# The first block of a second feed-forward as one paired product with two sevens, small loads behind a weight product, and five small groups of instructions a step later

## The chip, the cores and the metric

One core of one Trainium2 chip runs the kernel. The metric is the device time of one execution in microseconds (us): the median of repeated runs, 2222.22 us for the kernel before. The engines are written as the profile writes them: PE (matmul), PEld (weight load), DVE (vector), ACT (scalar), POOL (GpSimd) and SP (the queue that issues most DMAs). L345 is line 345 of the kernel before unless the text says otherwise.

## The reference, cut to what matters

A decoder layer on 256 tokens of width 2048 in fp32: a feed-forward (FFN1), a mixer of windowed attention and a recurrent branch, a cross-attention, a second feed-forward (FFN2), a final norm.

```python
def rms_norm(x, g):
    y = x * lax.rsqrt(jnp.mean(x * x, axis=-1, keepdims=True) + NORM_EPS)
    return y * g
def swiglu(h, w_gate, w_up, w_down):      # h 256x2048, gate and up 2048x5632, down 5632x2048
    return (jax.nn.silu(h @ w_gate) * (h @ w_up)) @ w_down
...
x = x + 0.5 * swiglu(rms_norm(x, g_ffn2), w_gate, w_up, w_down)
```

What the change touches most is the first 512 columns of `h @ w_gate` and `h @ w_up` of FFN2.

## The kernel before, in words

**Matmuls.** Every fp32 operand is split in two parts, hi (a cast on ACT, L345) and lo (what the cast left over, a subtraction on DVE, L346). One product of 128 rows takes three matmuls (`times`, L438 to L440): hi with xhi, lo with xhi, hi with xlo. The tokens stand in two halves t = 0, 1.

**Items.** A weight comes in items of 2 x 128 rows and 512 columns (`items`, with k = 2q the first row block). A plain item is 12 matmuls. A paired item carries the same rows of gate and up: 24 matmuls. `load` issues an item's DMA on SP, `divide` splits it, `next_item` loads up to `LOADED` ahead and divides up to `AHEAD` = 2 item costs ahead (a paired item costs two). The tiles hi and lo have 3 buffers each, so a cast waits until the item three tiles back has left PE. A raw tile is narrow (128x2x512, `raw`, 4 buffers) where no large pool is open, or wide (`raw2`, 128x4x512, `RAW` = 3 buffers).

**Sevens.** In some paired items (`SEVEN`) the eight products of the 2x2 block scheme become seven: 21 matmuls instead of 24. For that DVE forms sums of weights (`sums`, L365 to L367: one 128x1024 and two 128x512), ACT and DVE split them (thi L370 and tlo L371, twice each, 128x1024), and DVE and ACT form combinations c of the activations (`combinations`: u L470 and L475 to L480, chi L483, clo L486). After the last seven, DVE adds banks (`end`, L575 to L577), and the last items end with more adds (`finish`).

**Order of the work.** One Python program emits the instructions of all engines. Beside the weight stream run background generators in named groups (`Interleave`): a `tick` after each product advances each group by one step, and `idle(n)` skips n steps. A scheduler then fixes the order in each engine's row; each engine works its row in order. `issue_after(x)` (and `behind_weights`, which uses it) ties an instruction behind another.

**FFN2's opening, before.** Blocks of 512 columns: block 0 is a gate product and then an up product, each of 8 plain items (96 matmuls each), q = 0 to 7. The first four gate items are narrow, since FFN2's pool isn't open when they are loaded. Just ahead of it the cross-attention's output product ends (its matmuls read ochi, oclo), and the norm of its result `x` turns into the operands: `Norm.block` transposes four columns of x on PE (L187), writes xhi on ACT (L689) and xlo on DVE (L690), column by column, and squares x on ACT (`junk`, L698). After the last of four such groups, DVE sums the squares (`ms`, L752, L754) and POOL takes the root (rs, L756). Blocks 1 to 10 are paired with sevens (`gate_up`). Combinations c start when all of x is done.

**The five small groups.** In the attention: the sum of the softmax (`den`), and the point from which the transposed probabilities go on (the idle ahead of `pt`). In the recurrent branch: the decays' sigmoid chain (an idle of 4), the substitution that inverts a triangular matrix (`xt`, `tmp`, L1247 to L1255, on DVE and ACT), and the block inverse after it (n from ACT, L1388, feeds matmuls at L1351).

## Time and profile before

| | |
|---|---|
| three runs, median (lowest to highest) | 2222.22 us (2221.36 to 2223.51) |
| profiled execution | 2222.56 us |
| its span | 2220.8 us (1.76 us lie around it) |
| granted PE clock | 0.999 |
| matmuls recorded on PE | 10774 |
| bytes read from and written to HBM | 419.00 and 12.45 MB |

The span is one execution. In the lines of the timeline the first number is the start in us from the span's start, the second the duration in us, and brackets hold the idle time of that engine ahead of the instruction and what released it. Matmuls overlap: each record is some 0.39 us long, but the next starts 0.23 us later.

### The profile page before, as it was taken

What the parts mean: (1) busy time and instruction counts of PE and PEld (TensorE: products, weight loads), DVE (VectorE), ACT (ScalarE), POOL (GpSimd) and SP (SyncE); (2) the same over time, 40 slices, a digit from 0 to 9 for tenths busy, and PEclk for the clock granted to TensorE, in tenths of its full rate; (3) what the DMA queues carried; (4) which work ended last, traced back from release to release, by engine and by line L of the source; (5) the groups of instructions that cost most, each with busy time, mean ns of one, the idle gap of its engine ahead of it and who ended that gap; (6) DMA issues with size and microseconds to landing.
All of it is one profiled execution on the core that took longest, in us unless ns stands there. A gap on an engine that the chain in (4) does not pass through costs nothing.

```text
span 2220.8 us, 28313 instructions
## 1 busy us (share of the span) xinstructions
PE 2207.0 (99%) x10774; PEld 1817.7 (82%) x10774; DVE 1759.2 (79%) x2047; ACT 1193.8 (54%) x1438; POOL 72.0 (3%) x140
## 2 busy tenths in 40 slices
PE   9999999999999999999999999999999999999998
PEld 7788888888888877888888888888888888888886
DVE  8988988898887477878546576558888988898887
ACT  6555555555555557534434455456555555555554
POOL 1000000000000000010400000000000000000000
PEclk9999999999999999999999999999999999999999
DMA  7565665565556545677714665557565565565564
GB/s 266 200 219 193 204 208 190 190 209 192 206 183 217 169 131 159 210 226 224 203 55 146 229 219 202 187 168 259 199 204 184 200 209 190 189 208 193 205 207 154
DMA packets 220536, 433.31 MB, mean 195 GB/s; under 512 B 13952, under 2 KB 16336, under 8 KB 220400
## 3 DMA queue, kind: packets, MB, share of 16 engines
q1 hardware_dynamic: 213200, 410.70, 55.6%
q0 software_dynamic: 6624, 20.14, 2.9%
q8 instruction: 84, 1.38, 0.2%
q10 hardware_dynamic: 576, 0.66, 0.1%
q14 instruction: 52, 0.43, 0.1%
HBM read 419.00 MB, written 12.45 MB: 194 GB/s over the span
## 4 chain that ended last, share of the span: by engine, by line
PE 96%; DVE 1%; issue 1%; ACT 1%; DMA 0%; POOLq 0%; POOL 0%; SPq 0%; ACTq 0%; DVEq 0%
PE acc L438 21%; PE acc L439 20%; PE acc L440 20%; PE two L438 9%; PE two L439 9%; PE two L440 9%; PE two L187 2%; PE two L179 1%; DVE lo L346 1%; PE two L1351 0%; PE acc L1488 0%; PE acc L1453 0%; PE acc L1470 0%; PE two L1568 0%; PE acc L1351 0%
## 5 line engine op out<-in xcount | busy, mean ns | idle before, releaser
L345 ACT CAST hi<-raw 128x1024 fp32r<-128x1024 f32 (+1 forms) x769 | 764.0, 1003 | 794.3 <-PE two L440 370.6
L346 DVE TENSOR_TENSOR lo<-raw,hi 128x1024 fp32r<-128x1024 f32 (+1 forms) x770 | 884.2, 1158 | 325.0 <-ACT hi L345 323.7
L438 PE MATMUL acc<-hi,xhi 128*128 128x512 f32 (+1 forms) x1224 | 477.9, 391 | 1.1 <-ACT hi L345 0.7
L439 PE MATMUL acc<-lo,xhi 128*128 128x512 f32 (+1 forms) x1224 | 474.9, 388 | 0.9 <-DVE lo L346 0.9
L440 PE MATMUL acc<-hi,xlo 128*128 128x512 f32 (+1 forms) x1224 | 473.8, 387 | 0.0
L438 PEld LDWEIGHTS acc<-hi,xhi 128*128 128x128 f32 x1224 | 229.6, 188 | 53.3 <-issue 3.9
L439 PEld LDWEIGHTS acc<-lo,xhi 128*128 128x128 f32 x1224 | 229.8, 188 | 49.7 <-DVE lo L346 3.7
L440 PEld LDWEIGHTS acc<-hi,xlo 128*128 128x128 f32 x1224 | 229.8, 188 | 46.3 <-DVE xlo L712 0.2
L371 DVE TENSOR_TENSOR tlo<-raw,thi 128x1024 fp32r<-128x1024 f32 x160 | 193.1, 1220 | 0.0
L370 ACT CAST thi<-raw 128x1024 fp32r<-128x1024 f32 x160 | 165.8, 1051 | 33.4 <-DVE raw L365 19.1
L439 PE MATMUL acc<-lo,hhi 128*128 128x512 f32 x424 | 166.4, 392 | 0.0
L440 PE MATMUL acc<-hi,hlo 128*128 128x512 f32 x424 | 165.1, 389 | 0.0
L438 PE MATMUL acc<-hi,hhi 128*128 128x512 f32 x424 | 159.8, 391 | 0.1
L438 PE MATMUL two<-hi,xhi 128*128 128x512 f32 x352 | 138.4, 393 | 0.0
L439 PE MATMUL two<-lo,xhi 128*128 128x512 f32 x352 | 137.1, 390 | 0.0
L440 PE MATMUL two<-hi,xlo 128*128 128x512 f32 x352 | 137.0, 389 | 0.0
L365 DVE TENSOR_TENSOR raw<-raw 128x1024 f32<-128x1024 f32 x80 | 97.6, 1220 | 14.9 <-DMA raw<-in_ffn_w_up_dram 13.1
L439 PEld LDWEIGHTS acc<-lo,hhi 128*128 128x128 f32 x424 | 79.6, 188 | 19.3 <-DVE lo L346 3.1
L438 PEld LDWEIGHTS acc<-hi,hhi 128*128 128x128 f32 x424 | 79.1, 188 | 18.8 <-ACT hi L345 2.6
L440 PEld LDWEIGHTS acc<-hi,hlo 128*128 128x128 f32 x424 | 79.6, 188 | 16.3
L438 PEld LDWEIGHTS two<-hi,xhi 128*128 128x128 f32 x352 | 66.1, 188 | 15.0 <-DVE u L590 0.5
L440 PEld LDWEIGHTS two<-hi,xlo 128*128 128x128 f32 x352 | 66.1, 188 | 13.9
(392 smaller groups left out, 3190.2 us busy)
## 6 DMA issues: line engine op xcount, KB each, us to landing
raw<-in_ffn_w_gate_dram SPq DMA_DIRECT2D x171, 512.0 KB, 3.7
raw<-in_ffn_w_up_dram SPq DMA_DIRECT2D x167, 512.0 KB, 4.6
raw<-in_ffn_w_down_dram SPq DMA_DIRECT2D x152, 512.0 KB, 4.7
raw<-in_w_in_dram SPq DMA_DIRECT2D x136, 512.0 KB, 3.5
raw<-in_w_out_dram SPq DMA_DIRECT2D x32, 512.0 KB, 3.6
raw<-in_ffn_w_down_dram SPq DMA_DIRECT2D x12, 1024.0 KB, 5.1
raw<-in_w_proj_attn_dram SPq DMA_DIRECT2D x16, 512.0 KB, 3.6
raw<-in_w_proj_rwkv_dram SPq DMA_DIRECT2D x16, 512.0 KB, 4.2
```

The source lines that it names most:

```text
L179: prev = pe.matmul(to, lhs, rhs, **how)
L187: prev = pe.transpose(to, src, ident[:])
L345: newest["act"] = act.copy(hi[:, s], raw[:, s])
L346: newest["dve"] = dve.tensor_tensor(lo[:, s], raw[:, s], f32(hi[:, s]), ALU.subtract)
L365: dve.tensor_tensor(ta[:], raw[:, 1:3], raw[:, 0:2], ALU.subtract)
L370: act.copy(hi[:, s], t[:])
L371: dve.tensor_tensor(lo[:, s], t[:], f32(hi[:, s]), ALU.subtract)
L438: pe.matmul(o, xh, hi, start=first, stop=False, **how)
L439: pe.matmul(o, xh, lo, start=False, stop=False, **how)
L440: newest["pe"] = pe.matmul(o, xl, hi, start=False, stop=last, **how)
```

## The change

Six edits:

1. FFN2's block 0 becomes one paired product (`opening`) over gate and up in the order q = 1, 3, 5, 0, 6, 2, 7, 4, with sevens at q = 0 and 2. Its first item is loaded as two narrow tiles, all others as raw2. The combinations for FFN2 start without the six idle steps, in the order 0, 2, 4, 1, 3, with single idle steps.
2. `load` takes wide tiles whenever a pool is open, which also turns eight narrow loads of the mixer's first weight product into four wide ones.
3. `late_vectors` issues its three small DMAs inside `issue_after` of the newest matmul.
4. The attention: `den` a step later in one of its blocks, and another condition for idle 5 or 4 ahead of `pt`.
5. The decays' idle is 3 instead of 4; the copy of `tmp` (96x1024 on ACT) is split in two halves with a step between.
6. A step more after n in the block inverse.

```diff
+OPENING, SEVEN_OPENING = (1, 3, 5, 0, 6, 2, 7, 4), (0, 2)
@@ feed_forward_plan
-            if j == 0 and together:
-                yield (wg, wu), 0, KD, (0, 0), ()
-            elif j == 0:
-                for w in (wg, wu):
-                    yield w, 0, KD, 0, 512
+            if j == 0:
+                yield (wg, wu), 0, KD, (0, 0), () if together else SEVEN_OPENING
@@ late_vectors
+        with tc.issue_after(newest["pe"].ins):
+            pool.dma_start(gains[:], a["g_later"])
...
@@ load
+        if paired(i) and at["pool"] is None:
+            rows = slice(k * P, (k + KU) * P)
+            raws[i] = []
+            for v, c in zip(w, c0):
+                raw = wp.tile([P, KU, 512], F32, tag="raw", name="raw", bufs=4)
+                nc.sync.dma_start(
+                    raw[:], v[rows, c : c + 512].rearrange("(a p) n -> p a n", p=P)
+                )
+                raws[i].append(raw)
+            return
...
-        wide = at["pool"] is not None and (i < ends[0] or i >= ends[1] + LOADED)
+        wide = at["pool"] is not None
@@ combinations
-            for q in sorted(seven + early):
+            for q in seven + early if soon else sorted(seven + early):
...
-                yield from idle(2)
+                yield from idle(1 if soon else 2)
@@ product_pair
-        for q in range(late + 1):
+        for q in order:
@@ opening (new; product_pair calls after, end and finish)
+        def after(b):
+            act.copy(hb[:, 0], b["p1"])
+        def end(b):
+            dve.tensor_tensor(u[:, 0], b["p6"], hb[:, 0], ALU.add)
+            dve.tensor_tensor(u[:, 1], b["p7"], u[:, 0], ALU.add)
+            dve.tensor_tensor(u[:, 0], b["p5"], u[:, 0], ALU.add)
+            dve.tensor_tensor(u4[:], b["p5"], u[:, 1], ALU.add)
+        def finish(to, b):
+            bg.until(lambda: norm.r is not None)
+            t, v = to in ("p4", "p8"), plus[to]
+            if to in ("p2", "p4"):
+                dve.tensor_tensor(hb[:, t], b[to], v, ALU.add)
+                act.activation(hb[:, t], hb[:, t], AF.Silu, scale=norm.r[t])
+            else:
+                dve.tensor_tensor(v, b[to], v, ALU.add)
+                dve.scalar_tensor_tensor(hb[:, t], v, norm.r[t], hb[:, t], ALU.mult, ALU.mult)
+        product_pair(
+            x, c, w, True, SEVEN_OPENING, (), after, end, finish, order=OPENING
+        )
@@ softmax of the attention
-            yield
+            yield from idle(2 if qb and not kvs[0] else 1)
             dve.tensor_reduce(den[:], s3, AX.X, ALU.add)
...
-            yield from idle(5 if nk == 2 and kvs[0] else 4)
+            yield from idle(5 if kvs[0] > 1 else 4)
@@ decays
-                yield from idle(4)
+                yield from idle(3)
@@ after the substitution
-            act.copy(tmp[:96], xt[:96].rearrange("p u t -> p t u"))
+            for t in (slice(0, 16), slice(16, 32)):
+                act.copy(tmp[:96, t], xt[:96, :, t].rearrange("p u t -> p t u"))
+                yield
@@ block inverse
             act.copy(n2_[low].rearrange("p c n t -> p c (n t)"), b[low])
-            yield
+            yield from idle(2)
```

**ACT's row at the opening.** The rows below are ACT's in order. raw without a number is a narrow tile, raw_12262 and its like are wide ones. Before, from the cast of the second gate item (waiting for DMAHW0) to the casts of gate items 4 and 5 (raw_12262):

```order
L345 CAST hi<-raw 128x1024 [waits DMAHW0_49,PE_49]
L689 ACTIVATE xhi<-two,g_later 128x256 [waits DVE_49]
L345 CAST hi<-raw 128x1024 [waits DMAHW1_49,PE_49]
L689 ACTIVATE xhi<-two,g_later 128x256 [waits DVE_49]
L689 ACTIVATE xhi<-two,g_later 128x256 [waits PE_49]
L689 ACTIVATE xhi<-two,g_later 128x256 [waits DVE_49]
L698 ACTIVATE junk,ss<-x_10697 128x512 [waits Activation_49]
L689 ACTIVATE xhi<-two,g_later 128x256 [waits DVE_49]
L698 ACTIVATE junk,ss<-x_10697 128x512 [waits Activation_49]
L345 CAST hi<-raw 128x1024 [waits DMAHW2_49,PE_49]
L689 ACTIVATE xhi<-two,g_later 128x256 [waits DVE_49] x2
L698 ACTIVATE junk,ss<-x_10698 128x512 [waits Activation_49] x2
```

In the changed kernel (L356 is the cast, L734 xhi, L743 the squares), from the cast of the up half of the first item to the two casts of the second (raw_12252):

```order
L356 CAST hi<-raw 128x1024 [waits DMAHW4_49,PE_49]
L734 ACTIVATE xhi<-two,g_later 128x256 [waits DVE_49] x3
L743 ACTIVATE junk,ss<-x_10690 128x512 [waits Activation_49] x2
L734 ACTIVATE xhi<-two,g_later 128x256 [waits PE_49]
L734 ACTIVATE xhi<-two,g_later 128x256 [waits DVE_49] x3
L743 ACTIVATE junk,ss<-x_10691 128x512 [waits Activation_49] x2
L356 CAST hi<-raw_12252 128x1024 [waits DMAHW6_49,DMAHW5_49]
L356 CAST hi<-raw_12252 128x1024 [waits PE_49]
```

Two casts (those of gate items 2 and 3) have left the stretch, and the rest keeps its order: the next cast stands behind the last group's four xhi and two squares in both.

**DVE's row at the same place.** Changed kernel, from the sum of squares on (L797, L799 are ms, L357 lo, L376 to L378 the sums of weights, L382 tlo, L484 to L500 the combinations):

```order
L797 TENSOR_REDUCE ms<-ss 128x2 [waits Activation_49]
L799 TENSOR_SCALAR ms<-ms 128x2 [waits DVE_49]
L357 TENSOR_TENSOR lo<-raw_12252,hi 128x1024 [waits DMAHW6_49,DMAHW5_49,Activation_49]
L357 TENSOR_TENSOR lo<-raw_12252,hi 128x1024 [waits Activation_49]
L484 TENSOR_TENSOR u<-xhi,xlo 128x512
L489 TENSOR_TENSOR u<-u 128x128 [waits DVE_49]
L491 TENSOR_TENSOR u<-u 128x128
L490 TENSOR_TENSOR u<-u 128x128 [waits DVE_49]
L357 TENSOR_TENSOR lo<-raw_12255,hi 128x1024 [waits DMAHW7_49,DMAHW0_49,Activation_49]
L492 TENSOR_TENSOR u<-u 128x128 [waits DVE_49]
L484 TENSOR_TENSOR u<-xhi,xlo 128x512 [waits DVE_49]
L376 TENSOR_TENSOR raw<-raw_12258 128x1024 [waits DMAHW2_49,DMAHW1_49]
```

Before, from the same sum of squares on:

```order
L752 TENSOR_REDUCE ms<-ss 128x2 [waits Activation_49]
L754 TENSOR_SCALAR ms<-ms 128x2 [waits DVE_49]
L346 TENSOR_TENSOR lo<-raw_12262,hi 128x1024 [waits DMAHW3_49,Activation_49]
L346 TENSOR_TENSOR lo<-raw_12262,hi 128x1024 [waits Activation_49]
L470 TENSOR_TENSOR u<-xhi,xlo 128x512
L475 TENSOR_TENSOR u<-u 128x128 [waits DVE_49,Pool_49]
L477 TENSOR_TENSOR u<-u 128x128
L476 TENSOR_TENSOR u<-u 128x128 [waits DVE_49]
L346 TENSOR_TENSOR lo<-raw_12264,hi 128x1024 [waits DMAHW4_49,Activation_49]
L478 TENSOR_TENSOR u<-u 128x128 [waits DVE_49]
```

The two lo behind ms belong to plain items 4 and 5 before, and to the second paired item now; sums of weights, which before came 28 rows behind ms, now come in the tenth row behind it.

**PE's row.** Changed kernel, the end of the opening's first item and the start of its second (L452 to L454 are hi with xhi, lo with xhi, hi with xlo). The matmul that waits for ACT is the 25th of the opening and needs the first cast of raw_12252; the one that waits for DVE needs the first lo of it:

```order
L452 MATMUL acc<-hi,xhi 128x512
L453 MATMUL acc<-lo,xhi 128x512
L454 MATMUL acc<-hi,xlo 128x512
L452 MATMUL acc<-hi,xhi 128x512 [waits Activation_49]
L452 MATMUL acc<-hi,xhi 128x512
L453 MATMUL acc<-lo,xhi 128x512 [waits DVE_49]
L454 MATMUL acc<-hi,xlo 128x512
L453 MATMUL acc<-lo,xhi 128x512
L454 MATMUL acc<-hi,xlo 128x512
```

The eight transposes of the last group of x stand behind nine matmuls of the first item and ahead of 15; before, they stood behind seven matmuls of the gate product, and the matmul that needs the cast of raw_12262 was its 49th.

**Rows that stay.** POOL's three small DMAs of `late_vectors` stand at the same place of POOL's row in both kernels and wait for nothing in either (the named matmul is on another engine). Until the end of FFN1 all rows are the same.

More of the change, by code (lines that the diff above doesn't have):

```diff
@@ L289, in decoder_layer @@
         w, k0, nk, c0, n = entry
-        for q in range(nk // KU):
+        opens = len(ends) > 1 and len(items) == ends[1]
+        for q in OPENING if opens else range(nk // KU):
             items.append((w, k0 + KU * q, c0, n, isinstance(w, tuple) and q in n))
@@ L379, in divide @@
             parts[i] = split_raw(raw, WHOLE)
+        elif isinstance(raw, list):
+            g, u = (split_raw(v, WHOLE) for v in raw)
+            parts[i] = (g[0], u[0]), (g[1], u[1])
         elif items[i][4]:
@@ L399, in next_item @@
             room -= cost(j)
-            if room < 0 or (paired(j) and at["pool"] is None):
+            if room < 0 or (paired(j) and at["pool"] is None and j < ends[0]):
                 break
@@ L448, in multiply, with combinations @@
             )
-    def combinations(sp, x, seven, early, ready, tag, apart):
+    def combinations(sp, x, seven, early, ready, tag, apart, soon=False):
         n = 4 * len(seven) + 2 * len(early)
@@ L494, in combinations, with product_pair @@
         return c
-    def product_pair(x: Act, c, w, four, seven, early, after, end, finish, first=()):
+    def product_pair(x: Act, c, w, four, seven, early, after, end, finish, first=(), order=None):
         pw, _, nk, _, n = plan[at["product"]]
@@ L504, in product_pair @@
         at["product"] += 1
-        b, begun, late = {}, set(), nk // KU - 1
+        b, begun = {}, set()
+        order = order or range(nk // KU)
+        late, ends_seven = order[-1], [q for q in order if q in seven][-1:]
         def bank(to):
@@ L611, in first_block, with opening @@
         product_pair(x, None, w, False, (), (), None, None, finish)
+        return hb
+    def opening(sp, x, c, norm, w):
+        hb, u = (sp.tile([P, 2, 512], F32, tag="hb", name="hb", bufs=2) for _ in range(2))
+        u4 = sp.tile([P, 512], F32, tag="u", name="u", bufs=2)
+        plus = {"p2": hb[:, 0], "p4": u[:, 1], "p3": u[:, 0], "p8": u4[:]}
+        def after(b):
[17 more added lines that the diff above has]
+        )
         return hb
```

30 lines of the change are left out of this document (9 added, 21 removed).

## The prediction

> **What bounds the kernel now.** I read the page's busy times and its chain first, then what PE waits for, then the windows around FFN2's opening, and there the rows of each engine.
>
> ```profile
> PE 2207.0 (99%) x10774; PEld 1817.7 (82%) x10774; DVE 1759.2 (79%) x2047; ACT 1193.8 (54%) x1438; POOL 72.0 (3%) x140
> PE 96%; DVE 1%; issue 1%; ACT 1%; DMA 0%; POOLq 0%; POOL 0%; SPq 0%; ACTq 0%; DVEq 0%
> ```
>
> PE is busy 2207.0 of 2220.8 us, and 96% of the chain is PE. So a matmul less is a gain, and a gap on PE is a loss, one for one. What can be gained from gaps is small:
>
> ```profile
> PE two L187 <- ACT tok L907: 1.0, 2, 0.6
> PE acc L439 <- DVE lo L346: 0.9, 2, 0.6
> PE two L187 <- DVE s L980: 0.6, 1, 0.6
> PE two L1351 <- ACT n L1388: 0.2, 1, 0.2
> ```
>
> These are (total, times, longest) all waits that the five small groups could touch; none lies in FFN2's opening. The opening's own windows (busy times of PE, PEld, DVE, ACT, POOL, then the granted clock):
>
> ```profile
> core 0: us, PE busy (x) PEld busy (x) DVE busy (x) ACT busy (x) POOL busy (x), PEclk, DMA share, GB/s
> 1507.84:1551.40 43.56, 43.56 (x198) 36.16 (x197) 35.23 (x55) 27.53 (x40) 4.31 (x6) 1.00 0.76 270
> 1551.40:1573.20 21.80, 21.80 (x100) 17.64 (x99) 21.12 (x23) 12.56 (x14) 0.00 (x0) 1.00 0.59 200
> ```
>
> PE never stops in either, but DVE has 8.3 us to spare in the opening and 0.7 us in the block behind it, where two sevens lie. The change brings sevens into the opening, so DVE is what I follow.
>
> **Matmuls removed.** The opening falls from 192 to 186 matmuls.
>
> ```profile
> 1507.84 0.39 PE L438 MATMUL acc<-hi,xhi 128*128 128x512 f32 x1
> 1508.52 0.39 PE L438 MATMUL acc<-hi,xhi 128*128 128x512 f32 x1
> 1509.42 1.03 PE L187 MATMUL two<-ident,x 128*128 128x128 f32 x8
> 1510.21 0.48 PE L439 MATMUL acc<-lo,xhi 128*128 128x512 f32 x1
> ```
>
> Three matmuls start 0.68 us apart, 0.227 each: six are -1.36 us. Eight transposes take 0.79 us of PE.
>
> **The first wait it adds.** The opening starts at 1507.84. Before, plain items of 12 matmuls followed, and the cast of item 4 was needed only after 48. Now the first item has 24, and the second item's cast is needed at 1507.84 + 24 x 0.2267 + 0.79 = 1514.07. On ACT that cast still stands behind the last group's four xhi and two squares, and on DVE its lo behind ms:
>
> ```profile
> 1510.50 0.84 ACT L689 ACTIVATE xhi<-two,g_later 128x256 fp32r<-128x256 f32 x2 [1.04 <-PE two L187]
> 1515.55 0.47 ACT L689 ACTIVATE xhi<-two,g_later 128x256 fp32r<-128x256 f32 x1 [1.31 <-DVE xlo L690]
> 1515.92 0.62 ACT L698 ACTIVATE junk<-x 128x512 bf16<-128x512 f32 x1
> 1516.66 0.63 ACT L698 ACTIVATE junk<-x 128x512 bf16<-128x512 f32 x1
> 1517.29 1.98 ACT L345 CAST hi<-raw 128x1024 fp32r<-128x1024 f32 x2
> 1498.08 0.46 ACT L689 ACTIVATE xhi<-two,g_later 128x256 fp32r<-128x256 f32 x1
> 1499.09 0.47 ACT L689 ACTIVATE xhi<-two,g_later 128x256 fp32r<-128x256 f32 x1 [0.55 <-DVE xlo L690]
> ```
>
> ```profile
> 1517.42 0.16 DVE L752 TENSOR_REDUCE ms<-ss 128x2 f32<-128x8 f32 x1 [0.88 <-ACT junk L698]
> 1518.36 2.36 DVE L346 TENSOR_TENSOR lo<-raw,hi 128x1024 fp32r<-128x1024 f32 x2 [0.57 <-ACT hi L345]
> ```
>
> The last transposes now start after nine matmuls, at 1509.88 instead of 1509.42. The first xhi came 1.08 behind them (1510.50), so now 1510.96. Each xhi waits for the xlo ahead of it and starts 1.02 behind the last (1498.08, 1499.09): three steps give 1514.0 for the fourth. From the fourth xhi (1515.55) to the cast (1517.29) it was 1.74: the cast starts at 1515.76 and ends near 1516.8. Its lo began 1.07 behind the cast (1518.36): 1516.83 to 1518.05. That the two casts ahead of it are gone is in this sum. So PE waits 1514.07 to 1516.8, 2.75 us, runs two matmuls, and waits 0.75 more for lo: **3.5 us**. The loads aren't late:
>
> ```profile
> 1491.35 12.72 SPq L334 DMA_DIRECT2D raw<-in_ffn_w_gate_dram  x6
> ```
>
> SP issued six loads (4 MB) from 1491.35 to 1504.1, each as its tile came free. The first four items now (4 MB) wait for the same narrow tiles or for regions that were free before 1504.
>
> **DVE's backlog.** From there DVE has its row to work off. Start to start it takes 1.14 for 1024 columns (1559.61 to 1560.75), 0.60 for 512 (1563.02 to 1563.62):
>
> ```profile
> 1558.28 0.69 DVE L366 TENSOR_TENSOR raw<-raw,raw 128x512 f32<-128x512 f32 x1
> 1559.00 0.69 DVE L367 TENSOR_TENSOR raw<-raw,raw 128x512 f32<-128x512 f32 x1
> 1559.61 1.22 DVE L346 TENSOR_TENSOR lo<-raw,hi 128x1024 fp32r<-128x1024 f32 x1
> 1560.75 2.35 DVE L371 TENSOR_TENSOR tlo<-raw,thi 128x1024 fp32r<-128x1024 f32 x2
> 1563.02 0.68 DVE L346 TENSOR_TENSOR lo<-raw,hi 128x512 fp32r<-128x512 f32 x1
> 1563.62 1.22 DVE L365 TENSOR_TENSOR raw<-raw 128x1024 f32<-128x1024 f32 x1
> ```
>
> I count its row from that first lo (1516.83) to the first tlo of block 1's second seven. 1024 wide: 10 lo of five paired items, 4 each of the opening's two sevens and block 1's first, 2 lo, 3 up to that tlo, 1 hlo, together 28, or 31.9 us. 512 wide: 8 in sums of weights, 3 lo, 8 in combinations, 4 in end, 4 in finish, together 27, or 16.2. Two products with rs at 0.66, twelve subtractions at 0.21 and four operations on 256 columns at 0.34 are 5.2. The sum is 53.3: DVE is there at 1570.1, if it never waits. PE without any wait would need it after 234 matmuls and two sets of transposes: 1507.84 + 53.05 + 1.58 = 1562.5. So PE is held back by at least **7.6 us** there, the 3.5 included. Before, the same tlo ended at 1561.9 and was needed at 1563.8: the margin of 1.9 is what is eaten first. Walking the row item by item, PE stops some ten times for 0.2 to 1.2 us where a lo, a tlo or a bank that the adds of end read comes last, and DVE waits a few tenths for thi; I take **9.0**, with 6.5 and 10.5 as ends (DVE 3% quicker, or PE not making up what it lost between). Behind block 1's second seven DVE, by then freed of combinations and adds, is again ahead of PE, so nothing is given back and nothing more is lost.
>
> **The small groups.** Den a step later shortens the wait for s (0.6) by about 0.3; the idle ahead of pt only moves transposes beside weight matmuls. The waits for lo (0.9) stand ahead of any changed row and stay. The decays' idle moves one block by six matmuls, but the transposes of tok that wait (0.6 of the 1.0) and ACT's sigmoids ahead of them keep their places: 0. The split copy comes one cast earlier, and its first half frees ACT sooner: of the 0.4 left I take 0.3. The step after n: 0.2, and 0.2 for the shorter form switches there. Against it, the substitution's steps on DVE come one lo earlier in a stretch where DVE has nothing to spare:
>
> ```profile
> 985.00:1033.00 48.00, 48.00 (x213) 39.58 (x212) 47.11 (x63) 19.58 (x20) 0.73 (x1) 1.00 0.66 209
> ```
>
> I put 0.2 on that (bounds 0 and 0.9, the room that 47.11 of 48.00 leaves). Sum **-0.8**, bounds -1.8 (all waits listed but the lo) and +0.9. The small loads stand where they stood on POOL and wait for nothing: 0. Four wide loads for eight narrow ones at the mixer: PE waits for no DMA there; 0.
>
> **Sum.** -1.36 + 9.0 - 0.8 = +6.8 us on the profiled 2222.56, which lies 0.34 above the median of the runs shown: 2222.22 + 6.8 = **2229.0 us**.
>
> **Rivals.**
> *The casts keep ahead* (not slower): paired items and sevens run without a gap in block 1 and might here. Place: the 25th and 26th matmul; it needs the first lo of the second item by 1514.5, 3.5 us before the time worked out, and DVE's 53.3 us in 46. For it: block 1's 21.12 of 21.80. Against it: block 1 has no combinations, no opening squares, and starts with its casts done. Price: -1.36 - 0.8, 2220.1; with all the small waits gone 2218.4 or, with what I can't see, below 2217.8. 9%.
> *Only the first wait counts*: while PE stands, DVE catches up, and behind it has margin as before. Price 3.5 - 1.36 - 0.8, 2223.6. Against it: the count of 53.3 starts behind that wait. It holds if DVE's row is 4 us shorter than counted. 14%.
> *The clock falls in the wait*: PE's two waits lie 0.45 us apart, 3.5 us in all. If the granted clock halved for as long, matmuls at 0.45 instead of 0.227 would lose up to 1.75 us more, though DVE's backlog hides some: 2230.8. Against it: the clock is 0.999 over the span; but the longest wait of PE that this trace has is 1.1 us, so it can't exclude it:
>
> ```profile
> PE acc L204 <- POOL ones L199: 1.1, 1, 1.1
> ```
>
> [...] 8%.
>
> **Chances.** My forecast has 69%. The range 2224.8 to 2232.0 leaves out the first rival, most of the second and the tail beyond the clock's. A measurement of this kernel tells about 0.2% (4.4 us) from no change. Slower by more than that, above 2226.7: my forecast, the clock and a little of the second, 79%. Within: 17%. Faster: 4%.
>
> **What would show it.** Right: in the changed trace PE waits some 2.7 us for ACT's hi near 1514 and then 0.7 for DVE's lo; DVE is busy without a gap from 1517 to about 1570 (less what the small groups move the start); more waits for lo and tlo of 0.2 to 1.2 us up to block 1's second seven and none behind it; the clock stays near 1. Wrong: no wait of PE for hi near 1514 (then ACT's chain of xhi is quicker than 1.02 a step); gaps on DVE between 1520 and 1560 (then the count of its row is too long); a wait of SP's loads showing as PE's; waits of the substitution above 1 us around 975 to 1035.

## The result and the profile after

The changed kernel takes 2231.45 us (median of 6, 2228.85 to 2233.13) against 2221.81 us of the kernel before on the same chip (median of 6, 2220.93 to 2223.51): ratio 1.0042, 95% interval 1.0029 to 1.0055, so +9.6 us. The forecast was 2229.0 and its range 2224.8 to 2232.0. Its profiled execution took 2230.7 us, span 2229.0, 8.2 more than the span before.

In what follows "net" is the difference of medians to the kernel before. Line numbers are those of each kernel: in the changed one L356 and L357 are hi and lo, L452 to L454 the three matmuls, L734 and L735 xhi and xlo, L743 junk, L381 and L382 thi and tlo.

The page's busy times and chain, and what PE waits for (total, times, longest), of the changed kernel:

```profile
PE 2209.9 (99%) x10768; PEld 1817.1 (82%) x10768; DVE 1771.4 (79%) x2065; ACT 1198.3 (54%) x1444; POOL 71.3 (3%) x140
PE 93%; DVE 3%; DMA 1%; ACT 1%; issue 1%; SPq 0%; POOLq 0%; POOL 0%; ACTq 0%; DVEq 0%
```

```profile
PE acc L453 <- DVE lo L357: 3.8, 9, 0.8
PE acc L452 <- ACT hi L356: 3.3, 3, 2.5
...
PE two L1386 <- DVE mk L1478: 0.4, 1, 0.4
```

Six matmuls fewer were recorded, and yet PE's busy time rose by 2.9 us: some of its matmuls became slower (records of 0.63 us instead of 0.39 behind the wait for hi below). The waits for lo and hi rose from 1.6 to 7.1 us, and DVE's share of the chain from 1 to 3%. The 1% of DMA in the chain is the kernel's first loads and two single ones at 1650 and 1937, outside the part that the change touches most.

The opening in the timeline, PE first. Its first matmul starts at 1506.37 (1507.84 before). The 24 of the first item end with the row at 1512.52, then PE waits for the second item's hi:

```profile
1506.37 0.39 PE L452 MATMUL acc<-hi,xhi 128*128 128x512 f32 x1
...
1512.52 0.39 PE L454 MATMUL acc<-hi,xlo 128*128 128x512 f32 x1
1515.39 0.99 PE L452 MATMUL acc<-hi,xhi 128*128 128x512 f32 x2 [2.49 <-ACT hi L356]
1516.65 0.80 PE L453 MATMUL acc<-lo,xhi 128*128 128x512 f32 x1 [0.27 <-DVE lo L357]
1517.25 0.63 PE L454 MATMUL acc<-hi,xlo 128*128 128x512 f32 x1
1517.67 0.63 PE L453 MATMUL acc<-lo,xhi 128*128 128x512 f32 x1
```

From 1512.52 to 1515.39 is 2.87, 2.65 more than the usual 0.226; lo costs 0.68 more. Behind that the matmuls start 0.427 apart, at a granted clock of 0.50 (below). ACT and DVE in the same place:

```profile
1512.57 0.47 ACT L734 ACTIVATE xhi<-two,g_later 128x256 fp32r<-128x256 f32 x1 [0.55 <-DVE xlo L735]
1512.94 0.62 ACT L743 ACTIVATE junk<-x 128x512 bf16<-128x512 f32 x1
1513.68 0.63 ACT L743 ACTIVATE junk<-x 128x512 bf16<-128x512 f32 x1
1514.31 2.92 ACT L356 CAST hi<-raw 128x1024 fp32r<-128x1024 f32 x3
```

```profile
1515.37 2.36 DVE L357 TENSOR_TENSOR lo<-raw,hi 128x1024 fp32r<-128x1024 f32 x2 [0.57 <-ACT hi L356]
...
1569.18 2.35 DVE L382 TENSOR_TENSOR tlo<-raw,thi 128x1024 fp32r<-128x1024 f32 x2
```

The fourth xhi and both squares stand ahead of the cast, and DVE's row runs from 1515.37 to the first tlo of block 1's second seven, which starts at 1569.18 and is done at 1570.4. The windows (busy times, then granted clock) show both the wait with its clock and DVE's row:

```profile
1512.70:1515.40 2.70, 0.21 (x2) 0.01 (x1) 0.84 (x4) 2.67 (x7) 0.51 (x1) 1.00 0.41 143
1515.69:1519.11 3.42, 3.15 (x8) 1.97 (x7) 3.38 (x7) 1.55 (x2) 2.05 (x3) 0.50 0.53 159
1519.40:1560.00 40.60, 39.47 (x166) 29.91 (x164) 40.56 (x58) 23.87 (x28) 0.00 (x0) 1.00 0.66 216
```

The granted clock is 0.50 for 3.4 us behind the wait. From 1519.4 to 1560 DVE is busy 40.56 of 40.60 us, and PE, which had no gap there before, loses time in small waits. The last ones of them:

```profile
1557.14 0.50 PE L453 MATMUL acc<-lo,xhi 128*128 128x512 f32 x1 [0.54 <-DVE lo L357]
1560.67 0.50 PE L453 MATMUL acc<-lo,xhi 128*128 128x512 f32 x1 [0.83 <-DVE lo L357]
1562.50 0.33 PE L186 MATMUL two<-ident,hb 128*128 128x128 f32 x1 [0.17 <-DVE hb L652]
```

Behind these no wait belongs to the opening. The matmul that needs the tlo of 1569.18 starts at 1571.51, 1.1 us after that tlo is done, so the lo and the hb above are the last for which DVE held PE back on the opening's account. Summed up over PE's row (each start less the start ahead of it, less the usual distance of that shape, 0.226 for 512 columns), PE loses 4.8 us in the first 20 us of the opening and 5.0 in the next 40; before, 0.1 and 0.5. These two sums are worked out for each kernel below, and together they are called the lost time. A trace shows one execution: without sevens and with the early squares it lies 2.7 us above its kernel's median, with one seven 1.9, in the others at most 1.2 off.

### The profile page after: what moved, and what is told of

Same layout as the page of the kernel before. It is cut to its first block, busy times and chain, and to the rows that moved or that the text cites. A ratio compares the mean times of both kernels' runs of the same rounds, so it can differ in the third digit from the quotient of the medians.

```text
span 2229.0 us, 28322 instructions
## 1 busy us (share of the span) xinstructions
PE 2209.9 (99%) x10768; PEld 1817.1 (82%) x10768; DVE 1771.4 (79%) x2065; ACT 1198.3 (54%) x1444; POOL 71.3 (3%) x140
## 4 chain that ended last, share of the span: by engine, by line
PE 93%; DVE 3%; DMA 1%; ACT 1%; issue 1%; SPq 0%; POOLq 0%; POOL 0%; ACTq 0%; DVEq 0%
PE acc L452 20%; PE acc L453 20%; PE acc L454 20%; PE two L452 9%; PE two L453 9%; PE two L454 9%; PE two L186 2%; DVE lo L357 1%; PE two L178 1%; DMA raw<-in_ffn_w_up_dram 1%; DVE tlo L382 0%; PE two L1386 0%; PE acc L1523 0%; PE acc L1505 0%; PE acc L1488 0%
## 5 line engine op out<-in xcount | busy, mean ns | idle before, releaser
L356 ACT CAST hi<-raw 128x1024 fp32r<-128x1024 f32 (+1 forms) x769 | 762.4, 1001 | 785.8 <-PE acc L454 368.2
L357 DVE TENSOR_TENSOR lo<-raw,hi 128x1024 fp32r<-128x1024 f32 (+1 forms) x770 | 882.4, 1156 | 313.1 <-ACT hi L356 311.8
L452 PE MATMUL acc<-hi,xhi 128*128 128x512 f32 (+1 forms) x1200 | 468.8, 392 | 3.3 <-ACT hi L356 3.3
L453 PE MATMUL acc<-lo,xhi 128*128 128x512 f32 (+1 forms) x1200 | 466.7, 389 | 3.6 <-DVE lo L357 3.4
L454 PE MATMUL acc<-hi,xlo 128*128 128x512 f32 (+1 forms) x1200 | 465.1, 388 | 0.0
L452 PEld LDWEIGHTS acc<-hi,xhi 128*128 128x128 f32 x1200 | 225.2, 188 | 56.1 <-ACT hi L356 5.5
L454 PEld LDWEIGHTS acc<-hi,xlo 128*128 128x128 f32 x1200 | 225.7, 188 | 45.2
L382 DVE TENSOR_TENSOR tlo<-raw,thi 128x1024 fp32r<-128x1024 f32 x164 | 198.0, 1220 | 0.1
L381 ACT CAST thi<-raw 128x1024 fp32r<-128x1024 f32 x164 | 170.0, 1050 | 42.7 <-DVE raw L376 25.6
L454 PE MATMUL acc<-hi,hlo 128*128 128x512 f32 x424 | 165.1, 389 | 0.0
L452 PE MATMUL acc<-hi,hhi 128*128 128x512 f32 x424 | 159.8, 391 | 0.1
L452 PE MATMUL two<-hi,xhi 128*128 128x512 f32 x364 | 143.4, 394 | 0.0
L453 PE MATMUL two<-lo,xhi 128*128 128x512 f32 x364 | 141.9, 390 | 0.0
L454 PE MATMUL two<-hi,xlo 128*128 128x512 f32 x364 | 141.8, 389 | 0.0
L376 DVE TENSOR_TENSOR raw<-raw 128x1024 f32<-128x1024 f32 x82 | 100.1, 1220 | 17.3 <-DMA raw<-in_ffn_w_up_dram 14.9
L452 PEld LDWEIGHTS acc<-hi,hhi 128*128 128x128 f32 x424 | 79.1, 188 | 18.9 <-ACT hi L356 2.6
L454 PEld LDWEIGHTS acc<-hi,hlo 128*128 128x128 f32 x424 | 79.6, 188 | 16.2
L452 PEld LDWEIGHTS two<-hi,xhi 128*128 128x128 f32 x364 | 68.5, 188 | 15.5 <-DVE u L642 0.4
L454 PEld LDWEIGHTS two<-hi,xlo 128*128 128x128 f32 x364 | 68.4, 188 | 14.4
```

The source lines that it names most:

```text
L356: newest["act"] = act.copy(hi[:, s], raw[:, s])
L357: newest["dve"] = dve.tensor_tensor(lo[:, s], raw[:, s], f32(hi[:, s]), ALU.subtract)
L376: dve.tensor_tensor(ta[:], raw[:, 1:3], raw[:, 0:2], ALU.subtract)
L381: act.copy(hi[:, s], t[:])
L382: dve.tensor_tensor(lo[:, s], t[:], f32(hi[:, s]), ALU.subtract)
L452: pe.matmul(o, xh, hi, start=first, stop=False, **how)
```

## The experiments

The theory is the prediction's: **DVE's row** from the second item's lo to block 1's second seven sets the time. The first rival: **the first wait** and, since the trace shows it, **the half clock** behind it, which would cost PE whatever DVE does. The second: the pairing itself costs. For the small groups, the question is whether they give anything.

### The opening without sevens

```diff
-OPENING, SEVEN_OPENING = (1, 3, 5, 0, 6, 2, 7, 4), (0, 2)
+OPENING, SEVEN_OPENING = (1, 3, 5, 0, 6, 2, 7, 4), ()
...
-    def first_block(sp, x, norm, w):
+    def first_block(sp, x, norm, w, order=None):
...
-        product_pair(x, None, w, False, (), (), None, None, finish)
+        product_pair(x, None, w, False, (), (), None, None, finish, order=order)
...
-                hb = opening(sp, norm.x, c, norm, wg) if last else first_block(sp, norm.x, norm, wg)
+                hb = first_block(sp, norm.x, norm, wg, OPENING if last else None)
```

> The changed kernel with the opening paired and in the same order, but with no seven in it: 192 matmuls as before, and DVE without 4 sums of 512, 2 of 1024, 4 tlo and 6 adds of 512 columns, some 13 us. Against the kernel before. Theory (DVE's row sets the loss; without the 13 us it has caught up by 1556, long before 1563, so that only the first wait of 2.7 to 3.2 and its half clock of 0 to 1.5 are left, less 1.5 of the small groups): +1.2 to +3.5 us. Rival one (the pairing, the order or the loads cost, not the sevens): as the changed kernel and six matmuls more, +9.6 + 1.4 = +11.0. Rival two (the first wait is paid again later): near +6. In the trace: the first wait as in the changed kernel, no waits for lo, tlo or banks of over 0.2 between 1520 and 1570, gaps on DVE before 1560.

Measured: 2228.18 us, ratio 1.0029 (1.0018 to 1.0041), net +6.5 (+4.0 to +9.1). The theory's +1.2 to +3.5 is missed. All of PE's waits in the opening and block 1 that its timeline marks:

```profile
1517.03 0.73 PE L452 MATMUL acc<-hi,xhi 128*128 128x512 f32 x2 [2.48 <-ACT hi L356]
1518.28 0.50 PE L453 MATMUL acc<-lo,xhi 128*128 128x512 f32 x1 [0.53 <-DVE lo L357]
1559.58 0.50 PE L452 MATMUL two<-hi,xhi 128*128 128x512 f32 x1 [0.39 <-DVE hb L623]
1561.31 0.50 PE L453 MATMUL acc<-lo,xhi 128*128 128x512 f32 x1 [0.30 <-DVE lo L357]
```

```profile
1519.22:1522.63 3.41, 3.41 (x10) 2.62 (x9) 3.34 (x8) 0.43 (x1) 0.15 (x1) 0.50 0.91 273
1522.40:1540.00 17.60, 17.60 (x79) 14.58 (x78) 14.76 (x26) 9.41 (x12) 0.00 (x0) 0.99 0.79 271
```

As the theory said, DVE has time to spare now (14.76 of 17.60), and PE's small waits of 1520 to 1557 are gone. But the first wait stays. Its half clock lasts 3.4 us, as long as with sevens, but it begins behind the wait for lo and not ahead of it, so none of it is hidden there and it costs 2.0 us instead of 1.5. And two waits near 1560 are left: lost time 5.3 + 1.6, where two sevens lost 4.8 + 5.0. The theory's own terms, the first wait and its half clock, are 5.3 of these 6.9. Of the 3.0 us by which the theory missed its bound, 1.5 are what it credited to the small groups, which alone gave nothing (below); the rest lies in the half clock (2.0 in place of at most 1.5) and in the waits near 1560. Rival two's number, +6, is near, but not its mechanism: only 1.6 us come later. So with DVE ahead PE still loses 6.9 us, and with two sevens 9.8. That would fit two limits side by side, of which the longer counts; the next kernels test it.

### Matmuls in the first wait

Behind the first item's matmuls PE gets 12 more, into a bank that is begun anew later.

```diff
+            if fillers and q == order[0]:
+                bank("p1")
+                xh = x.parts[0][0]
+                for _ in range(fillers):
+                    with tc.issue_after(newest["pe"].ins):
+                        newest["pe"] = pe.matmul(
+                            b["p1"], xh[:, 4, :P], xh[:, 4:6, :].rearrange("p a n -> p (a n)"),
+                            start=True, stop=True,
+                        )
...
-            x, c, w, True, SEVEN_OPENING, (), after, end, finish, order=OPENING
+            x, c, w, True, SEVEN_OPENING, (), after, end, finish, order=OPENING, fillers=12
```

> The changed kernel with 12 matmuls more behind the first item of the opening, into a bank that the later products overwrite from the start, so that PE works on through the first wait and its granted clock has no cause to fall. Nothing is left out. Against the kernel before. Theory (DVE's row sets the time of block 1's second seven, and the 1.5 us that PE loses at half clock lie beside it): as the changed kernel, +9.6, within 0.5. Rival (the half clock adds its time to the end): 1.5 to 1.9 less, +7.7 to +8.1. In the trace: granted clock near 1 from 1512 to 1520 instead of 0.56 to 0.59; by the theory more PE waits for DVE between 1520 and 1570 to make up for it, by the rival the same ones.

Measured: 2231.27 us, ratio 1.0041 (1.0028 to 1.0054), net +9.6, as the changed kernel itself: the theory. The interval (+6.2 to +12.0) holds the rival's +7.7 to +8.1 too, so the trace has to tell. The windows:

```profile
1516.50:1520.00 3.50, 2.97 (x14) 2.40 (x14) 3.46 (x7) 1.46 (x3) 1.67 (x3) 1.00 0.64 186
1520.00:1540.00 20.00, 19.43 (x83) 14.87 (x82) 19.96 (x33) 11.61 (x16) 0.00 (x0) 1.00 0.72 233
```

The clock stays at 1.00, and the lost time in the first 20 us falls from 4.8 to 3.7 (1.0 beside the 12 matmuls' 2.7); in the next 40 it rises from 5.0 to 6.1. What the clock gave, a wait for DVE took: with two sevens the half clock lies beside DVE's row.

### One seven instead of two

```diff
-OPENING, SEVEN_OPENING = (1, 3, 5, 0, 6, 2, 7, 4), (0, 2)
+OPENING, SEVEN_OPENING = (1, 3, 5, 0, 6, 2, 7, 4), (2,)
```

> The changed kernel with one seven in the opening (q = 2) in place of two: three matmuls more (+0.68 us), and DVE without a sum of 1024, two of 512 and two tlo, some 4.6 us. Against the kernel before. Theory (DVE's row sets the loss, one for one as long as it is behind): 9.6 - 4.6 + 0.7 = +5.7 us, bounds +5.0 and +7.0. Rival (the number of sevens isn't what costs, but the adds at their end or the first wait): +9.6 + 0.7 = +10.3. In the trace: the first tlo of block 1's second seven some 4 to 5 us earlier than in the changed kernel (1569.18).

Measured: 2229.31 us, ratio 1.0032 (1.0020 to 1.0044), net +7.1. That is between the two and just above the theory's bound; the interval (+4.4 to +9.8) holds the theory's +5.7 too. In the profiled execution the first tlo of block 1's second seven starts at 1570.63, 62.4 behind the opening's start (1508.26), against 62.8 in the changed kernel, not 4 to 5 us earlier. DVE, with some 4.6 us less to do (the expectation's count), stands still instead:

```profile
1517.00:1540.00 23.00, 22.18 (x89) 17.92 (x90) 21.01 (x35) 12.38 (x15) 2.64 (x4) 0.93 0.65 213
1540.00:1570.00 30.00, 27.93 (x123) 21.82 (x122) 27.71 (x33) 16.33 (x20) 0.00 (x0) 1.00 0.61 206
```

DVE has 4.3 us free in 53, and PE still waits for a lo three times (lost time 5.3 + 3.4, where two sevens lost 4.8 + 5.0). One of DVE's waits is for a load:

```profile
1523.81 1.22 DVE L357 TENSOR_TENSOR lo<-raw,hi 128x1024 fp32r<-128x1024 f32 x1 [0.79 <-ACT hi L356]
1531.86 1.23 DVE L376 TENSOR_TENSOR raw<-raw 128x1024 f32<-128x1024 f32 x1 [0.76 <-DMA raw<-in_ffn_w_up_dram]
1543.17 0.50 PE L453 MATMUL acc<-lo,xhi 128*128 128x512 f32 x1 [0.97 <-DVE lo L357]
```

The chain that ended last runs from the matmuls at half clock to the cast that waits for them (1522.73), to its lo (1523.81), to the load that SP issues behind that lo (1525.06), and 6.3 us of DMA later to the seven's sum of weights (1531.86). From there DVE's row is full up to PE's wait at 1543.17. So "one for one" fell: in this execution PE's first loss comes back through a load, a tie that the count of DVE's row left out.

### Weight sums on POOL

```diff
-    def sums(raw):
+    def sums(raw, eng=None):
+        eng = eng or dve
-        dve.tensor_tensor(ta[:], raw[:, 1:3], raw[:, 0:2], ALU.subtract)
+        eng.tensor_tensor(ta[:], raw[:, 1:3], raw[:, 0:2], ALU.subtract)
...
-            t = sums(raw)
+            t = sums(raw, pool if ends[1] <= i < ends[1] + 8 else None)
```

> The changed kernel with the weight sums of the opening's two sevens (two of 1024 columns and four of 512, some 4.7 us of DVE) on POOL instead of DVE. Against the kernel before. Theory (DVE's row sets the loss): 9.6 - 4.7 = +4.9 us if POOL is ready in time; between +4.9 and +9.6 if POOL takes several times as long for them as DVE or slows DVE beside it; above +9.6 only if a thi waits for POOL longer than DVE saves. Rival (the sums are hidden): +9.6. In the trace: the first tlo of block 1's second seven up to 4.7 us earlier than 1569.18.

Measured: 2238.12 us, ratio 1.0071 (1.0059 to 1.0084), net +15.9. The expectation had a loss above +9.6 only for a thi that waits for POOL. DVE and POOL, side by side:

```profile
1518.26 3.07 DVE L485 TENSOR_TENSOR u<-xhi,xlo 128x512 f32<-128x512 f32 x1
...
1525.50 0.69 DVE L485 TENSOR_TENSOR u<-xhi,xlo 128x512 f32<-128x512 f32 x1
...
1535.91 3.33 DVE L357 TENSOR_TENSOR lo<-raw,hi 128x1024 fp32r<-128x1024 f32 x1
```

```profile
1518.38 2.39 POOL L377 TENSOR_TENSOR raw<-raw 128x1024 f32<-128x1024 f32 x1
...
1532.87 5.29 POOL L377 TENSOR_TENSOR raw<-raw 128x1024 f32<-128x1024 f32 x1 [8.89 <-DMA raw<-in_ffn_w_up_dram]
```

The same DVE operation takes 3.07 us beside POOL's first sum and 0.69 without one; a lo that takes 1.22 elsewhere takes 3.33. POOL's sum takes 2.39 or 5.29 for 1024 columns. By these times the sums were not taken off DVE but put in its way, and the run says nothing on the theory. PE's granted clock is halved twice here, for 3.4 us near 1518 and for 6.8 us from 1547 on (0.996 over the span, where the changed kernel has 0.998), which adds to the loss. That DVE operation started 0.12 us ahead of POOL's first sum (by POOL's spans, which are rough) and still took 3.07. What in the two engines' work makes the one longer isn't shown.

### The squares ahead of the last xhi

```diff
+            if n == 3 and self.early:
+                for t in range(2):
+                    act.activation(
+                        junk_t[:], src[:, t, :], AF.Square, accum_out=self.ss[:, t, n : n + 1]
+                    )
             b = feats(src)
...
+            if n == 3 and self.early:
+                self.r = rstd(self.ss[:])
+                return
             yield
...
-        n4 = Norm(g_ffn2)
+        n4 = Norm(g_ffn2, early=True)
```

> The changed kernel with the last two squares of the norm ahead of and between the last xhi on ACT, instead of behind them, and ms on DVE ahead of the last xlo: the same work, but the second item's cast no longer stands behind the squares, and its lo not behind ms. Against the kernel before. The wait for hi falls from 2.5 to about 1.4, and DVE starts its row 1.1 earlier. Theory (DVE's row sets the time from its start): 9.6 - 1.1 = +8.5 us, whatever the clock does. Rival one (the half clock costs in full, and a wait of 1.4 doesn't bring it): -1.1 - 1.5, +7.0. Rival two (the first wait is made up later, so its length is nothing): +9.6. In the trace: the cast of the second item near 1513.2 instead of 1514.31; the granted clock behind the wait near 1 or still near 0.6.

Measured: 2228.87 us, ratio 1.0033 (1.0020 to 1.0046), net +6.6. By its median that is nearest to rival one (+7.0), by its interval (+4.4 to +10.2) all three stand. The trace is of an execution 2.7 us above the median (+9.4). In it the wait for hi is 1.88 instead of 2.65, the clock is 1.00 behind it, and the lost time goes from 4.8 + 5.0 to 2.9 + 6.2. So 1.9 us were saved at the first wait, 1.2 of them came back as waits for DVE, and 0.7 is left, as much as DVE started earlier. That is the theory's reading, with 0.7 in place of 1.1, for this execution. Why the median is lower isn't shown.

### Without sevens: matmuls in the wait, and early squares

If there are two limits, the clock must count where DVE is ahead. The first of these two kernels puts the 12 matmuls into the opening without sevens, the second gives that opening the early squares; both edits are those shown above, together.

> The opening without sevens, with the 12 filler matmuls of the second experiment's kind behind its first item; nothing is left out. Against the kernel before. The opening without sevens measured +6.5 us; its trace has the waits of 2.65 and 0.69, then ten matmuls at 0.427 instead of 0.227 (about 2.2), and 1.0 us of waits near 1560. Theory (two limits: DVE's row with sevens, PE's own lost time without them; so here, where DVE is ahead, the half clock does cost): 6.5 - 2.2 = +4.3 us, bounds +3.5 and +5.2. Rival (the half clock is made good later in any case): +6.5. In the trace: granted clock near 1 between 1512 and 1522.

> The opening without sevens, with the last two squares ahead of the last xhi on ACT; nothing is left out. Against the kernel before. With sevens that cut the wait from 2.65 to 1.88 us and the clock stayed up. Theory: 6.5 - 0.8 - 2.2 = +3.5 us, bounds +2.7 and +4.5. Rival one (the clock falls here too, with a wait of 1.9): +5.7. Rival two (DVE's row or the order of the items is what costs, not the first wait): +6.5. In the trace: a wait of 1.9 for hi, one of 0.7 for lo, granted clock near 1 behind them.

Measured with the matmuls: 2227.46 us, ratio 1.0023 (1.0014 to 1.0032), net +5.2; with the early squares 2227.69, ratio 1.0023 (1.0014 to 1.0032), net +5.5. The first is at the upper bound of the theory and 1.3 below the opening without sevens, which the intervals (+3.1 to +7.1 and +4.0 to +9.1) don't separate. The traces do: its lost time is 1.0 + 1.5 beside 2.7 for the 12 matmuls, 5.2 in all, against 5.3 + 1.6. Here the saved half clock is not taken back, where with two sevens all of it was: the second limit is PE's own. The second kernel ran into its rival one. Its wait was 1.74, that with sevens 1.72, and yet the clock fell:

```profile
1514.33 0.73 PE L452 MATMUL acc<-hi,xhi 128*128 128x512 f32 x2 [1.74 <-ACT hi L356]
1515.58 0.80 PE L453 MATMUL acc<-lo,xhi 128*128 128x512 f32 x1 [0.52 <-DVE lo L357]
1516.18 0.63 PE L454 MATMUL acc<-hi,xlo 128*128 128x512 f32 x1
```

The same rows of the kernel with sevens and early squares:

```profile
1516.63 0.73 PE L452 MATMUL acc<-hi,xhi 128*128 128x512 f32 x2 [1.72 <-ACT hi L356]
1517.89 0.50 PE L453 MATMUL acc<-lo,xhi 128*128 128x512 f32 x1 [0.53 <-DVE lo L357]
1518.22 0.40 PE L454 MATMUL acc<-hi,xlo 128*128 128x512 f32 x1
```

Behind the wait of 1.74 the matmuls of the last two rows take 0.80 and 0.63 us, behind that of 1.72 they take 0.50 and 0.40: the clock fell in one execution and not in the other. What decides isn't shown.

### The five small groups alone, and all but them

The first kernel is the kernel before with edits 4, 5 and 6 of the change; the second is the changed kernel without these and without the small loads' tie.

> The kernel before with the five small groups of the change alone; its opening, its loads and its small loads stay. Against the kernel before. Theory (the opening's start moved from 1507.84 to 1506.37 by these groups): -1.5 us, bounds -0.8 and -1.8. Rival one (the 1.47 us are a jitter of one execution): 0, within 0.4. Rival two (a group a step later costs as much as it saves): +0.5 or more. In the trace: no stall near 1036.9 (0.754 before) and 1112.7 (0.378 before), that at 818.8 at 0.50 instead of 0.78, and a new one of 0.60 near 1160.

> The changed kernel with the five small groups and the small loads as they were before: the paired opening with two sevens and the wide loads alone. Against the kernel before. Theory (the opening alone costs, the small groups give 1.5 back): 9.6 + 1.5 = +11.1 us, bounds +10.0 and +12.0. Rival (the small groups are worth nothing, or cost): +9.6 or less. In the trace, against the changed kernel shifted by the later start: the same waits of PE (2.5 for hi, 0.3 for lo) and the same half clock behind them.

Measured: the groups alone 2222.57 us (11 runs), ratio 1.0003 (0.9994 to 1.0012), net +0.9; the opening with the wide loads 2231.51, ratio 1.0044 (1.0030 to 1.0057), net +9.8. So by the medians the opening is the whole of the change's loss, and the groups, forecast at -0.8, gave nothing. Both theories (-1.5 and +11.1) are missed: they credited the groups with all of the 1.47 us by which the opening starts earlier in the changed kernel. It starts 1.0 us earlier (1506.84) in the kernel without the groups, too. The stall near 1036.9, which the expectation laid to the groups, is missing there as well as with the decays' step alone, so that its absence isn't shown to be the groups' work. The stall at 1112.7 is gone and a new one near 1160 is there, as told. And PE waits for lo at 975 and 1008:

```profile
975.35 0.50 PE L439 MATMUL acc<-lo,yahi 128*128 128x512 f32 x1 [0.57 <-DVE lo L346]
```

```profile
973.77 0.16 DVE L1247 TENSOR_TENSOR tmp<-xt,dl 128x1 f32<-128x1 f32 x1 [5.03 <-DMA dl<-ld]
...
974.07 1.23 DVE L346 TENSOR_TENSOR lo<-raw,hi 128x1024 fp32r<-128x1024 f32 x1
```

DVE stands 5.03 us at the first operation of the substitution, for the DMA of dl, and a lo that PE needs is queued behind it. In the kernel before the same operation stands one lo later in DVE's row, and nothing was late:

```profile
970.73 1.23 DVE L346 TENSOR_TENSOR lo<-raw,hi 128x1024 fp32r<-128x1024 f32 x1 [1.50 <-ACT hi L345]
974.87 0.16 DVE L1247 TENSOR_TENSOR tmp<-xt,dl 128x1 f32<-128x1 f32 x1 [2.92 <-DMA dl<-ld]
```

### The decays' step, without and alone

```diff
-                yield from idle(4)
+                yield from idle(3)
```

That is the whole edit of the second kernel; the first has the other four groups and leaves this line as it was.

> The kernel before with four of the five small groups: the decays' idle stays 4. Against the kernel before. The trace of all five groups shows the first operation of the substitution one lo earlier in DVE's row, where it waits for dl's DMA, and PE waits 0.73 and 0.36 for the lo behind it. Theory (the decays' step alone moves it; without it the stalls of 0.75, 0.38 and 0.27 that the others take away are a gain, less 0.6 for mk near 1160 if that stays): -0.8 us, to -1.5 if it goes. Rival (the groups are worth nothing, with or without it): 0, within 0.4. In the trace: no wait for lo at 975 and 1008.

> The kernel before with the decays' idle 3 instead of 4, and nothing else. Against the kernel before. Theory (it moves the substitution ahead of a lo, as in the trace of all five groups): +0.7 to +1.9 us, by waits for lo of 0.7 to 1.6 near 975 and 0.3 near 1008. Rival (those waits are a jitter of the loads, since the changed kernel's own trace has none): 0, within 0.4.

Measured: four groups without the decays 2221.46 us, ratio 0.9995 (0.9986 to 1.0003), net -0.8; the decays alone 2223.89, ratio 1.0006 (0.9998 to 1.0015), net +1.7. Each median is where the theory put it, though neither interval excludes zero by itself. The waits near 975 are gone without the decays' step; the one alone has one wait of 0.63 at 1008 in its trace, and none near 975. That the changed kernel's own trace has none is a matter of the load: there dl's DMA let DVE go at 971.57, in the groups' trace at 973.77. Of the nine profiles with all five groups seven show it, with 0.65 to 1.58 near 975 or 0.3 near 1008. So by the medians one of the five groups took away what the other four gave.

### A mended order

```diff
             pool.dma_start(blk(x3d, n), x2[n][:])
+            if n == 3:
+                for i in (0, 1):
+                    load(ends[1] + i)
+                    divide(ends[1] + i)
             bg.spawn("feat", n4.block(n, x2[n]))
...
-OPENING, SEVEN_OPENING = (1, 3, 5, 0, 6, 2, 7, 4), (0, 2)
+OPENING, SEVEN_OPENING = (1, 3, 5, 0, 6, 2, 7, 4), (2,)
...
-                yield from idle(3)
+                yield from idle(4)
```

> The changed kernel with three edits: the second item of the opening is loaded narrow and cast ahead of the last group's xhi and squares on ACT (its two loads and its split are written ahead of that group), one seven (q = 2) in place of two, and the decays' idle at 4. Nothing is left out. Against the kernel before. Theory (what costs is the first wait with its half clock, and DVE's row behind it; here the cast stands ahead of what delayed it, DVE starts some 3 us earlier and has 4.6 us less to do): three matmuls fewer (-0.7), the groups without the decays (-0.8), waits near the end of the opening (0 to +2): -0.5 us, bounds -1.5 and +1.5. Rival one (a paired opening costs as such, as the two kernels without sevens and with a warm clock suggest, both at +5.1): +4 or more. Rival two (the cast moved ahead makes the last xhi, the combinations or the third item's cast late): +1.5 to +4, with a wait of PE for xhi, c or hi between 1515 and 1535. In the trace: no wait of over 0.7 for hi near 1512 and granted clock near 1.

Measured: 2224.00 us (11 runs), ratio 1.0009 (1.0000 to 1.0018), net +2.4 (0.0 to +4.0). That is above the theory's bound of +1.5 and below rival one. It is in rival two's range, but the wait of PE for xhi, c or hi between 1515 and 1535 that rival two asked for isn't there; the one there is for a lo. ACT's row shows that the second item's casts now come between the xhi:

```profile
1505.67 1.06 ACT L356 CAST hi<-raw 128x1024 fp32r<-128x1024 f32 x1 [1.32 <-PE acc L454]
1506.62 0.46 ACT L734 ACTIVATE xhi<-two,g_later 128x256 fp32r<-128x256 f32 x1
...
1510.88 1.04 ACT L356 CAST hi<-raw 128x1024 fp32r<-128x1024 f32 x1
1511.82 0.47 ACT L734 ACTIVATE xhi<-two,g_later 128x256 fp32r<-128x256 f32 x1
```

```profile
1519.13 0.50 PE L453 MATMUL acc<-lo,xhi 128*128 128x512 f32 x1 [0.57 <-DVE lo L357]
1554.21 0.50 PE L453 MATMUL acc<-lo,xhi 128*128 128x512 f32 x1 [0.84 <-DVE lo L357]
```

The first wait is gone, and these two are all that PE's timeline marks up to block 1's end. The lost time is 1.2 + 2.5. The pairing as such costs little, then: the place of one cast, one seven less on DVE and the decays' step together make 7.2 of the 9.6 us. The three edits went in together; taken alone, one seven less gave 2.5 and the decays' step cost 1.7, so some 3 would be left for the cast if they add up, which isn't shown. Less than the kernel before it isn't: three matmuls (0.7) don't pay for the two lo that still come late.

## Why the prediction was right, and where it wasn't

*The bound.* PE sets the time and a stall in the opening is lost for good: right. Behind block 1 PE's row comes 6.7 us later than before (the same matmul at 1590.8 and 1584.1), and the opening starts 1.47 earlier: the opening costs 8.2, and with the 1.36 of the matmuls removed 9.5 us are lost there (9.2 by the lost time, 9.8 less the 0.6 of before). That the span, too, is 8.2 longer is chance: the earlier start is made up for the most part by waits for lo near 1665 (0.7) and 1947 (0.55) behind single loads; the kernel with the groups alone, whose opening is the old one, has such a wait of 0.85 near 1659.

*Matmuls removed, -1.36.* 10774 to 10768, right.

*The first wait, 3.5.* Right in place, cause and size: 2.65 and 0.68, ACT's steps at 1.03, the cast at 1514.31 (forecast 1515.76, less the 1.47 by which the opening starts earlier). What it left out of the sum is the 1.5 us that the half clock behind it added. The sign "the clock stays near 1" was wrong.

*DVE's backlog, 53.3 us and 9.0 for PE.* The count runs to the end of block 1's second seven's first tlo: from 1515.37 to 1570.4 are 55.0 us, 1.2 of them waits for hb and hi, so the work is right to 1%. The loss, 9.5, is near the 9.0. But its parts came out as 4.8 at the first item and 5.0 behind it where 3.5 and 5.5 were written; that they nearly make up for each other is luck. The place was misread: 236 matmuls stand ahead of that tlo's, not 234, and in the kernel before it is needed at 1565.27, not 1563.8. So the margin there was 3.4 us and not 1.9, and the least loss by the same sum 7.2 and not 7.6. In the changed kernel PE comes to it 1.1 us after it is done: the row on DVE held PE back earlier, up to 1562.5. And the text spoke as though that row were the whole cause. It is one of two limits: without sevens, with DVE ahead, the loss is still 6.5. The second rival had the other limit too small: PE's own wait counts with the clock, 5.3 us in the first 20 of the opening without sevens, not 3.5.

*The clock.* As a forecast of the time this rival added up to 1.75 us to the sum; the clock fell, but with two sevens that cost nothing, as the 12 matmuls showed. That it halves, and for as long as the two waits (3.5 us), was the author's assumption: the trace of before, where PE's longest wait is 1.1 us and the clock 0.999, doesn't show it. In the changed kernel it stood at 0.50 for 3.42 us behind a wait of 2.49, without sevens for 3.41 behind one of 2.48; in each of the six profiles whose clock fell at the first wait it stood there for 3.4 us. It fell behind 1.74 us, too, and stayed at 1.00 behind 1.72.

*The small groups, -0.8.* This step failed. It put 0.2 on the substitution, with a bound of 0.9; measured are 0.65 to 1.58 and 0.3 in most executions, and a stall for mk near 1160 that it didn't have (0.4 idle by the row above, 0.6 from start to start). Together +0.9 (0.9994 to 1.0012) in place of -0.8. The step that failed is the substitution's term: DVE, moved one lo earlier, stood 5.03 us for a DMA ahead of a lo that PE needed.

*The sum.* Forecast +6.8, measured +9.6 (6.4 to 12.2 by the interval). By the medians the groups came out 1.7 above their forecast and the opening alone, forecast at +7.6 and measured at +9.8, 2.2 above its own. Together that is more than the 2.8 to be explained, so the two don't add up to better than 1.1 us. The traces show 8.2 to 8.4 for the opening, and the difference to 9.8 is within the interval (6.7 to 12.7). The small loads' tie and the wide loads were put at nothing; neither was tried by itself.

## What to carry to other kernels

Where two engines are close to the limit in one stage, work out the time that each would set alone and take the longer one: taking away one of two limits then gives only the difference, as the 12 matmuls (nothing) and one seven less (2.5 us by the medians) did here. Ask also what ties the two together: here a late cast made a load late, and the load DVE. Before a product is paired, look at what stands ahead of the second item's cast in the row of the engine that makes it: here two squares and an xhi that nobody needed yet. And an instruction of an engine that works its row in order and waits for a DMA (5.03 us for dl here) should not be moved ahead of one that the bounding engine needs, however short it is.

## What the runs showed of the hardware

The granted clock of the matmuls halved behind a wait of 2.49 us (0.427 instead of 0.226 between starts, 0.50 for 3.4 us; the same 3.4 us without sevens, behind 2.48), and behind one of 1.74 us in one execution, where it stayed up behind 1.72 us in another. Two DVE operations took several times as long beside POOL's sums: 3.07 instead of 0.69 us and 3.33 instead of 1.22. Not all did: the lo of 1533.27 and 1534.47, begun while POOL's second sum of 1024 columns ran (from 1532.87 on), took 0.68 for 512 columns and 1.22 for 1024, as elsewhere.
